# A planned hybrid decoder step: engine queues modelled as overlapping, ScalarE's order fixed too, raw buffers handed out, and the inner product of two heads taken in one copy

## The chip, the cores and the metric

The kernel runs on one core of one Trainium2 chip. The metric is the device time of one execution in microseconds. Before the change it is 3202.98 us, the median of three runs (3199.14 to 3204.49).

The core has engines that run side by side, each with its own queue that it works off in order: TensorE (PE, matrix multiplication into PSUM), VectorE (DVE), ScalarE (ACT), GpSimd (POOL), and SyncE (SP), which issues DMA transfers here. An instruction waits on semaphores for what it needs of other engines, and everything behind it in the same queue waits with it.

## What is computed

One layer of a decoder with a convolution branch and a recurrent branch, on 2048 prompt rows and 8 sampled sequences of 4 rows each, of width 1024. Cut to what matters here:

```python
h = rmsnorm(x, norm_g)
p = h @ w_in                                   # 1024 x 10368
u = cg * xin                                   # convolution branch, width 3
y_c = bg * (conv_w[0]*u[t-2] + conv_w[1]*u[t-1] + conv_w[2]*u[t]) * silu(zc)
# recurrent branch: 16 heads of 64, token shift by mu, then along the sequence, per head
sa = S @ -kk
S  = S * d + outer(sa, kk * a) + outer(v, k)
y  = S @ r
y_r = (groupnorm(y) * ln_w + ln_b + bonus) * silu(zr)
m = sigmoid(gc) * (y_c @ w_out_c) + sigmoid(gr) * (y_r @ w_out_r)
out = rmsnorm(x + m @ w_o, final_g)
```

The last rows of the convolution, of the shift and the states S are returned as well.

## The kernel before, in words

**Tiles and stages.** The prompt is cut into 4 sets of 512 columns (tokens). The input lies with the features on the partitions as a high and a low part (`XH`, `XL`, fp32r); each weight block of 128 columns is split in the same way into `whl`: ACT casts the raw block `wraw` to the high part, DVE subtracts to get the low part. A projection of one block (`proj`) is then 24 matmuls of up to 512 columns, high by high, low by high and high by low, into the PSUM tile `ip`. These are the main stream of PE, some 11,700 matmuls. The split weights are stored to DRAM the first time and loaded split afterwards. A last stage computes the output projections (tiles `RH`, `RL`, `MH`, `ML`, `po`).

**The recurrence in chunks.** Heads are treated in pairs, with head 0 on partitions 0 to 63 and head 1 on 64 to 127. For each of 8 pairs and each set, the 512 tokens are 8 chunks of 64. Within a chunk, the recurrence is solved with the inverse of a triangular matrix per head. `rwkv_solve` finds inverses of 32x32 blocks by 62 short DVE operations (tiles `tt`, `X`, `Mi`), and `rwkv_merge` puts them together in `Xbd`, which before is block-diagonal: head h on rows 64h and columns 64h. `rwkv_chain` then goes through the chunks one after another. For each chunk:

1. PE: `pa` = the state `S` times `AR`.
2. DVE, two operations of 64x64: `us` = `pa` + `P1`, one for each head, stacked on the rows in a tile of 128x64.
3. PE: `pb[:, 0, 0:64]` = `Xbd` times `us`. Head 0 comes out on partitions 0 to 63 and head 1 on 64 to 127.
4. `inner`: DVE copies head 0 into `SV[0:64, c, 0:64]`, and ACT copies head 1 into `SV[0:64, c, 64:128]`.
5. PE: `pb[:, 1]` = `BKt` times `SV`.
6. DVE, two operations: the new `S`. ACT has scaled the old one into `sp` meanwhile.

Each step needs the one before it, and the next chunk needs `S`. There are 4 x 8 x 8 = 256 such chunks.

**What sets the order.** The chains, inverses, key computations and so on are generators, called sides (`Side`), which a driver mixes into PE's main stream: after each main matmul, `drive` asks each side to go on. A side gives out its next step when a model of the engines says that its inputs are ready (`self.due <= clock.t["PE"]`). This model is `Clock`: `add` gives each instruction a start and an end, from costs in `Traced.cost`, from when its inputs are ready, and from a gap in its engine's list of busy times (`gap`). At the end of the first stage the instructions of the engines in `PLANNED`, DVE alone before, are sorted by the starts that the model gave, and are tied together in that order. On the other engines the instructions stand as the framework lists them.

**Buffers.** `wraw` is a ring of 4 buffers of 512 KB, used in turn for raw weights, for rows of `x` and some more. `tmp` is a ring of 8 that are freed by name, and the model takes the one that it expects to be free first. Early in the program, `late_setup` brings the rows of `x` of the later sets through the `wraw` ring, while the first weights come through it too.

Of the kernel before, what the change touches and what calls it, by code (L numbers as in the profile page):

```python
# [16 lines left out]
P = 128  # L17
# [30 lines left out]
PLANNED = ('DVE',)  # L48


class Clock:
# [3 lines left out]
    def __init__(self):  # L55
        self.t = dict.fromkeys(("PE", "DVE", "ACT", "POOL", "SP"), 0.0)
        self.log, self.home = {}, {}
        self.mode = (128, 128)
        self.busy = {"DVE": [], "ACT": [], "POOL": []}
        self.touched = {}  # L60
        self.begun, self.planning = {}, False
        self.held = {"DVE": [], "POOL": []}
# [11 lines left out]
    def pool(self, pool, name, bufs):  # L74
# [9 lines left out]
        def free(k):  # L84

            return max((e[5] for i in range(k) for e in self.log.get(f"{name}{(n[0] + i) % bufs}", ())), default=0.0)
# [39 lines left out]
    def add(self, eng, outs, ins, cost, lag=60.0):  # L126
        start = max([self.t["PE"] - PAST if eng in self.busy else self.t[eng]] + [e[4] for ap in ins for e in self._hits(ap) if e[6] != eng] +
                    [e[5] for ap in (*ins, *outs) for e in self._hits(ap) if e[6] == eng] +
                    [self.touched.get((eng, ap.tensor.name), 0.0) for ap in (*ins, *outs)] +
                    [e[5] for ap in outs for e in self._hits(ap)])  # L130
        if eng in self.busy:
            start = self.gap(eng, start, cost)
        if eng == "POOL" or eng == "DVE" and sum(ap.space != PSUM for ap in ins) > 1:
            for _ in range(3):
# [4 lines left out]
                start = self.gap(eng, start, cost)  # L139
# [6 lines left out]
        if eng in self.busy:  # L146
# [4 lines left out]
            b.insert(i, (start, end))  # L151
            del b[:-200]
        self.t[eng] = max(self.t[eng], end)
        for ap in ins:
            for e in self._hits(ap):
                e[5] = max(e[5], end)
        for ap in outs:
            for p0, p1, f0, f1 in self.boxes(ap):
                old = self.log.setdefault(self.name(ap), [])
                old[:] = [e for e in old if not (p0 <= e[0] and e[1] <= p1 and f0 <= e[2] and e[3] <= f1)][-95:]  # L160
                old.append([p0, p1, f0, f1, end + lag, end, eng, start])
        return start


class Ring:
# [9 lines left out]
    def tile(self, shape, dtype, name, bufs=None):  # L175
        if name != "tmp":
            home, t = name, self.pool.tile(shape, dtype, name=name, bufs=bufs)
        else:
            home = min(self.open, key=self.ends)
# [4 lines left out]
        self.clock.log[home] = [[0, P, -1 << 40, 1 << 40, at, at, None, at]]  # L184
# [8 lines left out]
class Pooled:  # L193
# [3 lines left out]
    def tile(self, shape, dtype, name, bufs=None):  # L197
# [4 lines left out]
        if log:  # L202
            at = max(e[5] for e in log)
            self.clock.log[home] = [[0, P, -1 << 40, 1 << 40, at, at, None, at]]
        return t


class Traced:
# [5 lines left out]
    def __getattr__(self, op):  # L214
        f = getattr(self.eng, op)

        def call(*a, **k):
# [8 lines left out]
            if self.clock.planning and self.name in PLANNED:  # L226
# [4 lines left out]
    def cost(self, op, out, ins, k):  # L231
# [24 lines left out]
        if self.name == "DVE":  # L256
            per = {"transpose": 1.12 if n <= 256 else 1.86, "tensor_tensor_scan": 2.1, "reciprocal": 6.1}.get(op, 1.05)
            if op == "tensor_reduce":
                n = ins[0].free_size()
            one = op == "scalar_tensor_tensor" and isinstance(k["scalar"], bass.AP)  # L260
            return 145 + per * n + 58 * one
        if self.name == "ACT":
            strided = n > 64 and list(ins[0].ap)[-1][0] > 1
            return (155 if ins[0].space == PSUM else 190) + (1.9 if strided else 0.84) * n + 100 * max(0, len(ins) - 1) + 30.0
# [32 lines left out]
def hybrid_kernel(tc, x_prompt, x_sample, state_conv, state_shift, state_rwkv, norm_g, w_in, conv_w,  # L297
# [26 lines left out]
    wraw_p = clock.pooled(ctx.enter_context(tc.tile_pool(name="wraw", bufs=4)), "wraw", 4)  # L324
# [17 lines left out]
    def w_advance(dma, split, load):  # L342
        while state["dma"] < min(dma, len(order)):
            _, src, _, there = order[state["dma"]]
            if not there:
                raw = wraw_p.tile([P, NB * P], F32, name="wraw")
# [79 lines left out]
    class Side:  # L426
# [15 lines left out]
        def run(self, upto, force=False):  # L442
            if any(not x.ended for x in self.after) or upto < self.f0:
                return
            goal = weight[self.kind] * (upto - self.f0) / max(1e-9, self.f1 - self.f0) if upto < self.f1 else float("inf")
            while self.given < goal and self.f0 <= upto and (force or max(self.due, pt_free(self.banks)) <= clock.t["PE"] and (
                    self.kind in URGENT or clock.load("DVE") < BACKLOG)):
                try:
                    x = next(self.g)
                    x, aps, self.banks = (x + ((), 0)[len(x) - 1:]) if isinstance(x, tuple) else (x, (), 0)  # L450
# [3 lines left out]
                    self.due = clock.ready(aps) if aps else 0.0  # L454
                except StopIteration:
                    weight[self.kind] = self.given
# [3 lines left out]

    def need(*sides):
# [28 lines left out]
    def load_x(i):  # L490
        xt = wraw_p.tile([P, D], F32, name="wraw")
# [28 lines left out]
    tmp = Ring(ph1.enter_context(tc.tile_pool(name="tmp", bufs=1)), [P, NT + 64], 8, clock)  # L520
    ep = clock.pooled(ph1.enter_context(tc.tile_pool(name="ep", bufs=2)), "ep", 2)
# [13 lines left out]
    XB = [xp.tile([P, NC1, P], F32, name=f"Xbd{i}") for i in range(2)]  # L535
    SV = xp.tile([P, NC1, P], F32, name="SV")
# [1232 lines left out]
```

## Time and profile before

| | before |
|---|---|
| median of three runs | 3202.98 us |
| the profiled execution, its own time | 3202.88 us |
| its span in the trace | 3201.2 us |
| mean granted clock of TensorE | 0.993 |
| bytes moved by DMA | 615.07 MB, 192 GB/s over the span |
| first stage, to the last chunk of the recurrence | about 2640 us of the span |

The program records every operation through one helper, so nearly all rows of the profile carry the line L218, and a row is told from another by its tiles: `pb<-us,Xbd` is the matmul that writes `pb` from `us` and `Xbd`. An f32 matmul of the kernel is two passes in the trace, so 256 chunks show as 512 rows. "PEld" is the weight load, which runs beside the matmuls. A wait such as "PE pb <- ACT SV" means that PE stood idle before a matmul into `pb` until ACT had written `SV`.

### The profile page before, as it was taken

The page shows a single profiled execution, that of the slowest core. Times are in us where ns is not written, and L with a number is a line of the kernel's source. Part 1 is how long each engine was busy: PE and PEld are TensorE (multiplying, and loading weights), DVE is VectorE, ACT ScalarE, POOL GpSimd, SP SyncE. Part 2 cuts the span into 40 slices and gives each one's busy share as a digit, 9 for nine tenths or more (in the row PEclk, how much of TensorE's full clock was granted, in tenths as well). Part 3 has the DMA queues.
Part 4 walks back from the last instruction along what each step waited for, and adds up shares of the span by engine and source line. Part 5 has one row for each costly group of instructions (what it writes and reads, how often), then busy time and mean ns, then how long its engine had stood idle before and what let it go on. Part 6 is the DMA issues. An engine that isn't in the chain of part 4 may idle for free.

```text
span 3201.2 us, 55474 instructions
## 1 busy us (share of the span) xinstructions
PE 3095.1 (97%) x21530; PEld 2598.3 (81%) x21530; DVE 2000.1 (62%) x5704; ACT 1251.9 (39%) x2571; POOL 312.7 (10%) x517
## 2 busy tenths in 40 slices
PE   7899999999999999999999989999999999999998
PEld 6677777887777778777777789989899988877896
DVE  5677787866666666665666666777677763443332
ACT  5454555444443443444434334334444442311201
POOL 2011111011111111111111110000000000000000
PEclk9999999999999999999999999999999999999999
DMA  7776777654444444444444444334443468988863
GB/s 252 237 238 219 223 230 243 218 178 155 153 158 161 159 159 150 169 159 154 160 154 160 157 133 147 134 124 141 139 147 124 147 217 306 358 327 317 317 243 120
DMA packets 241501, 615.07 MB, mean 192 GB/s; under 512 B 33930, under 2 KB 143619, under 8 KB 187478
## 3 DMA queue, kind: packets, MB, share of 16 engines
q1 hardware_dynamic: 241094, 611.00, 55.9%
q8 instruction: 170, 2.79, 0.4%
q14 instruction: 93, 0.76, 0.1%
q0 software_dynamic: 144, 0.52, 0.0%
HBM read 452.10 MB, written 159.36 MB: 191 GB/s over the span
## 4 chain that ended last, share of the span: by engine, by line
PE 71%; DVE 16%; ACT 4%; issue 4%; DMA 4%; POOL 1%; SPq 0%; ACTq 0%; DVEq 0%; POOLq 0%
PE ip L218 51%; PE pt L218 10%; PE po L218 6%; DVE tt L218 3%; DVE X L218 3%; PE pb L218 3%; ACT tmp L218 2%; DVE Mi L218 2%; DVE tmp L218 2%; PE pa L218 1%; DVE us L218 1%; DVE S L218 1%; DMA wraw<-in_w_in_dram 1%; DVE whl L218 1%; ACT Xbd L218 1%
## 5 line engine op out<-in xcount | busy, mean ns | idle before, releaser
L218 PE MATMUL ip<-XH,whl 128*128 128x512 f32 (+3 forms) x7776 | 2106.6, 351 | 32.0 <-DVE whl L218 14.0
L218 PEld LDWEIGHTS ip<-XH,whl 128*128 128x128 f32 x7776 | 1341.3, 190 | 204.1 <-issue 39.4
L218 PE MATMUL ip<-XL,whl 128*128 128x512 f32 (+3 forms) x3888 | 1363.6, 351 | 2.4 <-DVE XL L218 2.0
L218 PEld LDWEIGHTS ip<-XL,whl 128*128 128x128 f32 x3888 | 738.7, 190 | 80.0 <-issue 7.7
L218 DVE TENSOR_TENSOR X<-X,tt 128x60 f32<-128x60 f32 (+24 forms) x992 | 213.2, 215 | 33.8
L218 DVE TENSOR_TENSOR tt<-Mi,X 128x60 f32<-128x60 f32 (+24 forms) x992 | 213.3, 215 | 27.5
L218 DVE SCALAR_TENSOR_TENSOR S<-pb,pe,sp 64x64 f32<-64x64 f32 x512 | 144.0, 281 | 108.5 <-PE pb L218 103.0
L218 ACT ACTIVATE sp<-S,pe 128x128 f32<-128x128 f32 x256 | 100.0, 401 | 244.5 <-DVE S L218 243.4
L218 ACT ACTIVATE tmp<-ip,vec 128x512 f32<-128x512 f32 (+2 forms) x174 | 103.2, 593 | 229.4 <-PE ip L218 228.0
L218 DVE TENSOR_TENSOR us<-pa,P 64x64 f32<-64x64 f32 x512 | 110.3, 215 | 127.7 <-PE pa L218 118.0
L218 PE MATMUL po<-whl,MH 128*128 128x512 f32 x544 | 170.3, 394 | 0.0
L218 ACT COPY SV<-pb 64x64 f32<-64x64 f32 x256 | 53.6, 209 | 292.7 <-DVE SV L218 290.8
L218 DVE TENSOR_TENSOR whl<-wraw,whl 128x1024 fp32r<-128x1024 f32 x105 | 130.9, 1248 | 20.7 <-ACT whl L218 20.4
L218 ACT CAST whl<-wraw 128x1024 fp32r<-128x1024 f32 x105 | 109.5, 1045 | 82.7 <-DMA wraw<-in_w_out_r_dram 45.1
L218 PEld LDWEIGHTS pb<-SV,BKt 128*128 128x128 f32 x512 | 81.3, 188 | 64.2 <-ACT SV L218 58.7
L218 PE MATMUL ip<-RH,whl 128*128 128x512 f32 (+2 forms) x512 | 128.4, 341 | 1.2 <-DMA whl<-w_or 0.9
L218 PE MATMUL pb<-SV,BKt 128*128 128x128 f32 x512 | 111.2, 299 | 17.5 <-ACT SV L218 16.6
L218 PEld LDWEIGHTS po<-whl,MH 128*128 128x128 f32 x544 | 102.2, 188 | 23.8
L218 DVE TENSOR_TENSOR GM<-pt,mask_p 128x512 f32<-128x512 f32 x128 | 82.5, 686 | 59.3 <-PE pt L218 59.2
L218 PEld LDWEIGHTS pb<-us,Xbd 128*128 128x128 f32 x512 | 86.5, 188 | 35.4 <-PE ip L218 17.0
L218 DVE SCALAR_TENSOR_TENSOR gt<-gt,ip 128x288 f32<-128x288 f32 (+2 forms) x67 | 36.5, 544 | 116.7 <-PE ip L218 102.7
L218 PE MATMUL po<-whl,ML 128*128 128x512 f32 x272 | 107.1, 394 | 0.0
(494 smaller groups left out, 3862.5 us busy)
## 6 DMA issues: line engine op xcount, KB each, us to landing
wraw<-in_w_in_dram SPq DMA_DIRECT2D x81, 512.0 KB
whl<-w_k SPq DMA_DIRECT2D x24, 1024.0 KB
whl<-w_r SPq DMA_DIRECT2D x24, 1024.0 KB
whl<-w_v SPq DMA_DIRECT2D x24, 1024.0 KB
whl<-w_z SPq DMA_DIRECT2D x24, 1024.0 KB
whl<-w_xin SPq DMA_DIRECT2D x24, 1024.0 KB
whl<-w_cg SPq DMA_DIRECT2D x24, 1024.0 KB
whl<-w_zc SPq DMA_DIRECT2D x24, 1024.0 KB
```

Source lines behind the costliest of these rows:

```text
L218: r = f(*a, **k)
```

## The change

Five things change.

- **The model of the queues.** `OVERLAP` lets an instruction of DVE or ACT occupy its engine for less than its duration when its output begins at partition 0, and for more when it does not. The wait for another engine before a buffer is overwritten gets 60 ns; that for the own engine's result is `e[4] - 26`. Some costs of `Traced.cost` change (ACT loses 30 ns; DVE's `tensor_scalar` from SBUF is 0.587 ns an element).
- **The fixed order.** `PLANNED` now holds ACT as well. Operations of the kinds in `LOOSE` (the preparation of `x`, the late setup, and the subtraction of the low part of a weight) are no longer tied, on either engine.
- **Buffers.** `Raws` hands out the four `wraw` buffers by name, as `tmp` is; they are freed where their last reader has been recorded. When no `tmp` is open, `push` forces sides on.
- **The chain.** `Xbd` holds the inverses of both heads in columns 0 to 63, head h still on rows 64h. `us` becomes block-diagonal, in two fixed tiles `UB` of 128x128 whose other blocks stay zero. The product then gives both heads on partitions 0 to 63 in 128 columns, and one ACT copy of 64x128 replaces the DVE copy and the ACT copy of 64x64. The samples' `inner` stays as it was.
- **Small things.** `rst` becomes bf16, and the last rows for `new_shift_p` are handled later in `prep`.

```diff
-PLANNED = ('DVE',)
+PLANNED = ('DVE', 'ACT')
+LOOSE = ('prep', 'first', 'late', 'zero', 'low')
+OVERLAP = {"DVE": (83, 13), "ACT": (60, 18)}
...
     def add(self, eng, outs, ins, cost, lag=60.0):
...
-                    [e[5] for ap in (*ins, *outs) for e in self._hits(ap) if e[6] == eng] +
+                    [e[4] - 26.0 if eng in OVERLAP else e[5] for ap in (*ins, *outs) for e in self._hits(ap) if e[6] == eng] +
                     [self.touched.get((eng, ap.tensor.name), 0.0) for ap in (*ins, *outs)] +
-                    [e[5] for ap in outs for e in self._hits(ap)])
+                    [e[5] + 60.0 * (e[7] != eng) for ap in outs for e in self._hits(ap)])
+        took = cost
+        if eng in OVERLAP:
+            over, drain = OVERLAP[eng]
+            p0 = self.boxes(outs[0])[0][0]
+            took = cost - over if p0 == 0 else cost + over + 2 * drain
         if eng in self.busy:
-            start = self.gap(eng, start, cost)
+            start = self.gap(eng, start, took)
...
+class Raws:
+    def __init__(self, pool, size, n, clock):
+        self.pool, self.clock, self.size = pool, clock, size
+        self.open, self.out = [f"wraw{i}" for i in range(n)], {}
...
+    def tile(self):
+        home = min(self.open, key=self.ends)
+        self.open.remove(home)
+        t = self.pool.tile([P, self.size], F32, name="wraw", tag=home)
...
-            if self.clock.planning and self.name in PLANNED:
+            if self.clock.planning and self.clock.kind not in LOOSE and self.name in PLANNED:
                 self.clock.begun.setdefault(self.name, []).append((at, r.ins))
...
-    wraw_p = clock.pooled(ctx.enter_context(tc.tile_pool(name="wraw", bufs=4)), "wraw", 4)
+    wraw_p = Raws(ctx.enter_context(tc.tile_pool(name="wraw", bufs=1)), NB * P, 4, clock)
...
+            was, clock.kind = clock.kind, "low"
             V.tensor_tensor(out=hl[:, 1], in0=raw, in1=hl[:, 0].bitcast(F32), op=ALU.subtract)
+            clock.kind = was
+            wraw_p.free(raw)
...
+    def push():
+        for sd in [sd for kind in ("samp", "keys", "out") for sd in live if sd.kind == kind and sd.f0 <= where[0]]:
+            if all(x.ended for x in sd.after):
+                sd.run(where[0] + 1e-6, True, True)
+                if tmp.open:
+                    return
...
+    UB = [xp.tile([P, P], F32, name=f"UB{i}") for i in range(2)]
...
-    rst = con.tile([P, NT], F32, name="rst")
+    rst = con.tile([P, NT], BF16, name="rst")
...
+    col = [slice(32 * b, 32 * b + 32) for _ in range(2) for b in range(2)]
...
-            A.copy(Xbd[g, 0:NCH, g].rearrange("p c (a e) -> p c a e", e=4),
+            A.copy(Xbd[g, 0:NCH, col[i]].rearrange("p c (a e) -> p c a e", e=4),
...
-                us = sm.tile([P, 64], F32, name="us")
+                us = UB[c % 2]
                 for h in range(2):
-                    V.tensor_tensor(out=us[HS[h]], in0=pa[0:64, c - g, HS[h]], in1=P1[HS[h], c, :], op=ALU.add)
+                    V.tensor_tensor(out=us[HS[h], HS[h]], in0=pa[0:64, c - g, HS[h]], in1=P1[HS[h], c, :], op=ALU.add)
...
-                inner(c, pb[:, 0], us, Xbd)
+                T.matmul(pb[:, 0, :], lhsT=Xbd[:, c, :], rhs=us, start=True, stop=True)
+                A.copy(SV[0:64, c, :], pb[0:64, 0, :])
```

Three places show what this does to the order. The first is PE's queue in the chain of the second set, some 1004 us into the program, from the product with the inverse (`pb<-us,Xbd`, afterwards `pb<-UB,Xbd`) to the next product of that chunk (`pb<-SV,BKt`). Before:

```order
2980 L218 MATMUL pb<-us,Xbd_209 128x64
2981 L218 MATMUL ip<-XH,whl 128x512 x2
2982 L218 MATMUL ip<-XL,whl 128x512
2983 L218 MATMUL ip<-XH,whl 128x512 x2
2984 L218 MATMUL ip<-XL,whl 128x512
2985 L218 MATMUL ip<-XH,whl 128x512
2986 L218 MATMUL pb<-SV,BKt 128x128
```

The same chunk in the changed program:

```order
2966 L264 MATMUL pb<-UB_210,Xbd_209 128x128
2967 L264 MATMUL ip<-XH,whl 128x512 x2
2968 L264 MATMUL ip<-XL,whl 128x512
2969 L264 MATMUL ip<-XH,whl 128x512 x2
2970 L264 MATMUL ip<-XL,whl 128x512
2971 L264 MATMUL pb<-SV,BKt 128x128
```

Six main matmuls stand between the two products where there were seven. The right side is 128 columns wide instead of 64.

The second place is ACT's queue at the same chunk; `cv<-u,cwh` is a step of the convolution that needs `u` from DVE, and `sp<-S,pe` is the scaling of the old state. Before:

```order
725 L218 ACTIVATE tmp<-tmp 128x512
726 L218 COPY SV<-pb 64x64
727 L218 ACTIVATE sp<-S_474,pe 128x128
728 L218 ACTIVATE cv<-u,cwh 128x512
729 L218 COPY SV<-pb 64x64
730 L218 ACTIVATE sp<-S_474,pe 128x128
```

In the changed program:

```order
729 L264 ACTIVATE tmp<-tmp 128x512
730 L264 ACTIVATE sp<-S_476,pe 128x128
731 L264 COPY SV<-pb 64x128
732 L264 ACTIVATE cv<-u,cwh 128x512
733 L264 ACTIVATE sp<-S_476,pe 128x128
```

The copy of this chunk (the second `SV<-pb` of the first list) has moved from behind the convolution's step to ahead of it.

The third place is DVE's queue in the first set, during the first inverse, where the low part of a weight is made (`whl<-wraw,whl`). Before, at the end of the inverse:

```order
149 L218 TENSOR_TENSOR tt<-Mi,X 128x24
150 L218 TENSOR_TENSOR X<-X,tt 128x8x3
151 L218 TENSOR_TENSOR tt<-Mi,X 128x16
152 L218 TENSOR_TENSOR X<-X,tt 128x8x2
153 L218 TENSOR_TENSOR tt<-Mi,X 128x8
154 L218 TENSOR_TENSOR X<-X,tt 128x8
155 L218 TENSOR_TENSOR whl<-wraw,whl 128x1024
156 L218 STREAM_TRANSPOSE Xo<-X 128x256
```

In the changed program, in the middle of that inverse:

```order
125 L264 SCALAR_TENSOR_TENSOR kT<-ip,omu,tmp 128x512
126 L264 TENSOR_TENSOR tt<-Mi,X 128x65
127 L264 TENSOR_TENSOR whl<-wraw,whl 128x1024
128 L264 TENSOR_TENSOR X<-X,tt 128x5x13
129 L264 TENSOR_TENSOR tt<-Mi,X 128x60
130 L264 TENSOR_TENSOR X<-X,tt 128x5x12
131 L264 TENSOR_TENSOR tt<-Mi,X 128x66
132 L264 TENSOR_TENSOR whl<-wraw,whl 128x1024
```

The subtraction, no longer tied to a planned place, has moved from behind the whole inverse into it.

Over the whole program the counts by operation are the same but for these: 256 DVE copies `SV<-pb` are gone, 256 ACT copies `SV<-pb` are 64x128 instead of 64x64, 256 matmuls into `pb` have 128 columns instead of 64, and POOL sets two tiles `UB` to zero at the start.

More of the change, by code (lines that the diff above doesn't have):

```diff
@@ L138, in add @@
                         start = e
-                start = self.gap(eng, start, cost)
+                start = self.gap(eng, start, took)
                 if start == was:
@@ L150, in add @@
                 i -= 1
-            b.insert(i, (start, end))
+            b.insert(i, (start, start + took))
             del b[:-200]
@@ L178, in tile @@
         else:
+            for _ in range(60):
+                if self.open:
+                    break
+                self.push()
             home = min(self.open, key=self.ends)
@@ L259, in cost @@
                 n = ins[0].free_size()
+            if op == "tensor_scalar" and ins[0].space != PSUM:
+                per = 0.587
             one = op == "scalar_tensor_tensor" and isinstance(k["scalar"], bass.AP)
@@ L699, in prep @@
                 to_cols(q, xt, (i - th * TPS) * P, G if k % 2 else V)
+                if q == NB // KG - 1 and i < NTL - 1:
+                    wraw_p.free(xt)
                 yield 1
@@ L717, in late_setup @@
             stat_tile(i, xt, m)
+            if i < NTL:
+                wraw_p.free(xt)
             yield 1
```

77 lines of the change are left out of this document (52 added, 25 removed).

## The prediction

> **What bounds the kernel now.** I read the page first, for the busy shares and the chain that ended last.
>
> ```profile
> span 3201.2 us, 55474 instructions
> PE 3095.1 (97%) x21530; PEld 2598.3 (81%) x21530; DVE 2000.1 (62%) x5704; ACT 1251.9 (39%) x2571; POOL 312.7 (10%) x517
> ...
> PE 71%; DVE 16%; ACT 4%; issue 4%; DMA 4%; POOL 1%; SPq 0%; ACTq 0%; DVEq 0%; POOLq 0%
> ```
>
> TensorE is busy for 97% of the span, so 106 us of it are open idle time (3201.2 - 3095.1). No other engine comes near. Whatever gains here must take work from PE or let it wait less. The program's count of matmuls does not change, so it comes down to waits. A busy PE can hide part of a wait, because pipelined matmuls overlap in the records; the weight loads therefore belong beside it. The view of the waits, for the matmuls and for the weight loads:
>
> ```profile
> PE pb L218 <- ACT SV L218: 16.6, 42, 2.1
> PE ip L218 <- DVE whl L218: 14.0, 6, 6.1
> ...
> PE pb L218 <- DVE us L218: 6.9, 21, 0.4
> ...
> PE pa L218 <- DVE S L218: 1.4, 2, 1.1
> PEld pb L218 <- ACT SV L218: 58.7, 140, 2.5
> ```
>
> Each row gives the total in us, how often, and the longest. The recurrence's chain is the largest single cause: for 140 of its 256 chunks the weights `SV` come late, 58.7 us together, of which 16.6 us are open idle time of PE. Next is the wait for a weight's low part, 14.0 us in six places, one of them of 6.1.
>
> What such a late `SV` costs is seen in one chunk of the timeline (start, duration, engine, instruction; "x2" are two passes or two matmuls):
>
> ```profile
> 1002.67 0.40 PE L218 MATMUL ip<-XL,whl 128*128 128x512 f32 x1
> 1002.90 0.38 PE L218 MATMUL pa<-S,AR 128*128 128x128 f32 x2
> 1003.04 0.71 PE L218 MATMUL ip<-XH,whl 128*128 128x512 f32 x2
> 1003.59 0.40 PE L218 MATMUL ip<-XL,whl 128*128 128x512 f32 x1
> ...
> 1004.53 0.33 PE L218 MATMUL pb<-us,Xbd 128*128 128x64 f32 x2
> 1004.66 0.71 PE L218 MATMUL ip<-XH,whl 128*128 128x512 f32 x2
> 1004.82 0.68 DVE L218 TENSOR_TENSOR u<-ip,tmp 128x512 f32<-128x512 f32 x1
> 1005.21 0.39 PE L218 MATMUL ip<-XL,whl 128*128 128x512 f32 x1
> ...
> 1005.42 0.21 DVE L218 COPY SV<-pb 64x64 f32<-64x64 f32 x1
> ...
> 1005.54 0.73 ACT L218 ACTIVATE cv<-u,cwh 128x512 f32<-128x512 f32 x1 [3.46 <-DVE u L218]
> ...
> 1006.14 0.40 PE L218 MATMUL ip<-XH,whl 128*128 128x512 f32 x1
> 1006.17 0.20 ACT L218 COPY SV<-pb 64x64 f32<-64x64 f32 x1
> ...
> 1006.41 0.30 PEld L218 LDWEIGHTS pb<-SV,BKt 128*128 128x128 f32 x2 [0.31 <-ACT SV L218]
> 1006.41 0.49 PE L218 MATMUL pb<-SV,BKt 128*128 128x128 f32 x2
> ...
> 1006.66 0.48 PE L218 MATMUL ip<-XH,whl 128*128 128x512 f32 x1
> ```
>
> The product `pb<-us,Xbd` ended at 1004.86 (1004.53 + 0.33). DVE was in `u` and copied only at 1005.42. ACT then took `cv<-u`, which its queue had ahead and for which it had stood idle 3.46 us, and copied at 1006.17. PE began at 1006.41 and the next main matmul at 1006.66. An undisturbed step takes 0.23 from the main matmul before it (1002.67 to 1002.90) and 0.14 to the one behind (1002.90 to 1003.04); here these are 0.27 and 0.25. So a wait of 0.31 in the weight load cost PE 0.15, and about 0.16 of each wait is hidden. Over all 140: 58.7 - 140 x 0.16 = 36 us lost, my estimate, between the bounds 16.6 and 58.7.
>
> **The change part by part.** The sum is made against the profiled execution's own 3202.88 us, which is the median (3202.98) within 0.1 us.
>
> *The copy of SA.* The groups of the two copies, and of a wider copy from PSUM on ACT:
>
> ```profile
> L218 DVE COPY SV<-pb 64x64 f32<-64x64 f32 x256 | 52.8, 206 | 57.7 <-PE pb L218 57.6
> L218 ACT COPY SV<-pb 64x64 f32<-64x64 f32 x256 | 53.6, 209 | 292.7 <-DVE SV L218 290.8
> L218 ACT COPY BKt<-pt 128x128 f32<-128x128 f32 x8 | 2.1, 267 | 0.1
> ```
>
> ACT's copy follows DVE's: its idle time ends with DVE's copy for 290.8 of 292.7 us. The change removes 256 copies of 206 ns from DVE and from the step, and widens ACT's from 64 to 128 columns, 209 to at most 267 ns: 0.15 us a step shorter. The planner gives that back: on PE's queue shown with the change, six main matmuls stand where seven stood, 0.23 us less cover. So the shorter step is worth nothing by itself; what counts is that one queue fewer can be late. In the chunk above, DVE's lateness was 0.56 us (1004.86 to 1005.42) and ACT's 0.54 (1005.63 to 1006.17). The first goes with the DVE copy; the second goes where the fixed order of ACT puts the copy ahead of `cv`, as its queue now has it. ACT is busy 39% of the time against DVE's 62%, so what is late next is an ACT evacuation of up to 0.6 us ahead of the copy. I take two thirds of 36 us as gained: **-24**, between 0 (all given back) and -58.7.
>
> *The right side, 128 instead of 64 columns.* In the timeline above, `pa` with 128 columns and `us` with 64 can be compared: from the first pass to the start of the third main matmul behind it, `pa` takes 1002.90 to 1003.59 = 0.69 and `us` 1004.53 to 1005.21 = 0.68, each with two main matmuls in it. So the wider side costs 0.01 a chunk, **0** (at most 3 us over 256). Its upper bound is the pass itself: the two passes' common duration is 0.38 against 0.33, the second pass starting 0.05 later; if both passes paid this, 256 x 2 x 0.05 = 26 us.
>
> *The sums `us` on DVE.* Their number and size stay, two 64x64 operations. The waits for them:
>
> ```profile
> L218 PEld LDWEIGHTS pb<-us,Xbd 128*128 128x128 f32 x512 | 86.5, 188 | 35.4 <-PE ip L218 17.0 <-issue 6.4 <-DVE us L218 0.3
> ```
>
> PE loses between 6.9 us (its idle row above) and 35.4. DVE has 52.8 of 2000.1 us less to do, and the planner's starts for DVE change with the overlap. I take **-4**, with +10 to -20 as ends, since a new order can also be a worse one.
>
> *The low part of a weight, and the raw buffers.* This is the 6.1 us wait:
>
> ```profile
> 110.83 0.39 PE L218 MATMUL pa<-S,AR 128*128 128x128 f32 x2
> ...
> 116.05 1.22 DVE L218 TENSOR_TENSOR whl<-wraw,whl 128x1024 fp32r<-128x1024 f32 x1
> ...
> 117.33 0.80 PE L218 MATMUL ip<-XH,whl 128*128 128x512 f32 x1 [6.11 <-DVE whl L218]
> 117.92 0.63 PE L218 MATMUL ip<-XL,whl 128*128 128x512 f32 x1
> 118.35 1.05 PE L218 MATMUL ip<-XH,whl 128*128 128x512 f32 x2
> 119.20 0.63 PE L218 MATMUL ip<-XL,whl 128*128 128x512 f32 x1
> 119.63 1.05 PE L218 MATMUL ip<-XH,whl 128*128 128x512 f32 x2
> 120.48 0.43 PE L218 MATMUL ip<-XL,whl 128*128 128x512 f32 x1
> 120.75 0.63 PE L218 MATMUL ip<-XH,whl 128*128 128x512 f32 x2
> ```
>
> DVE made this low part only when the whole inverse was through, since its fixed order had it there; and after the wait PE runs at about half speed to 120.75: eight main matmuls from 117.33 take 3.42 us, where 8 x 0.23 = 1.84 is usual, so 1.6 us more. With the change the low part stands in the middle of the inverse. Of 6.1 + 1.6 us I take **-6**. The raw buffers themselves I cost at nothing: they decide when a load may start, and the weights' loads keep their rank before the rows of `x` in SP's queue or gain one. If a row of `x` now holds a weight back there, the six waits of 14.0 us double; so +14 to -14.
>
> *ACT's fixed order elsewhere.* Weight loads also wait for other ACT results; the longest are 8.3 us for `tmp` and 7.5 for `Wm`. I take **-2**, with the sign open:
>
> ```profile
> PEld pt L218 <- ACT tmp L218: 8.3, 19, 1.4
> ...
> PEld pt L218 <- ACT Wm L218: 7.5, 20, 0.7
> ```
>
> `rst` in bf16, two POOL memsets and the later `new_shift_p` lie beside PE's stream, on engines at 62% and 10%; without that cover they are a few us at most.
>
> Sum: -24 + 0 - 4 - 6 - 2 = -36, and 3202.88 - 36 = **3167 us**.
>
> **The rivals.** *The planner takes it all back.* It places the product as soon as its model says that `SV` is ready, so a shorter step brings an earlier product and as many waits. The 0.23 taken from the cover speaks for this; the two lateness terms of the chunk, which the model did not foresee, speak against. Left are the 6 us at the start: 3197, and up to 3204.
>
> *All waits of the chain go.* Two queues foreseen well would free PE of nearly everything: -45 for `SV`, -15 for `us`, -10 at the start, -6 elsewhere: 3127. Against it stands DVE, still 60% busy and still in two steps of three.
>
> *Slower: ACT's queue is blocked by a weight.* The 81 casts of raw blocks of `w_in` (1.05 us each) are ACT instructions of the main stream and are tied now. Such a cast waits for a DMA, whose landing the model only guesses. Where the block is late, the copies `SV` and the evacuations of `ip` queue behind it and PE stops within the six matmuls of cover. It decides from a mean lateness of 36 / 81 = 0.44 us per cast on; at 0.7 us it is +57 - 36, or 3224. The trace of before shows ACT waiting long for a raw block only where the last stage begins:
>
> ```profile
> ACT whl L218 <- DMA wraw<-in_w_out_r_dram: 45.1, 2, 39.3
> ```
>
> *The wide side costs what its columns cost.* At the bound of 26 us the forecast becomes 3193. The two distances of 0.69 and 0.68 speak against it. A rule that says the same: the Trainium skill, "TensorE: Matmul & The Clock Gate", section "Back-to-back issue gap", gives about 60 cycles for up to 64 columns and 134 for 128, and "FP8 and Floating Point Precision", section "TensorE Precision Notes", four passes for full fp32; an estimate from these is 74 cycles at 2.4 GHz x 4 x 256 = 32 us, or 3199. The trace disagrees as far as it goes, since `pa` already has 128 columns at no more than `us` with 64.
>
> **How the numbers follow.** Forecast (3150 to 3185): 0.56. Planner takes it back: 0.17. All waits go: 0.12. ACT blocked: 0.09. Width costs: 0.06. A measurement of this kernel can tell about 0.2% from no change, which is 3196.6 to 3209.4. Faster is the forecast, all waits, half of the planner's case and most of the width's: 0.80; the same 0.11; slower 0.09, nearly all from ACT. The range has to hold eight in ten: up to 3204, the planner's upper end, and down to 3138, which takes in part of the larger gain and leaves the slower case out.
>
> **What would show it.** Right, if the weight loads' wait for `SV` falls from 58.7 to about 20 us with some 50 waits, the 6.1 us wait near 117 us is below 3, and the distance from `pb<-UB,Xbd` to the third main matmul behind it stays at 0.68 to 0.69. The planner's case shows as a wait for `SV` that stays near 58.7. The blocked case shows as ACT idle before `whl` on a DMA in the first stage, followed by waits of PE for ACT. The width's case shows in the distance alone. The forecast is wrong if DVE's new order makes the waits for `us` or `S` grow by more than what `SV` gives.

## The result and the profile after

The changed kernel takes 3172.86 us, the median of four runs (3170.4 to 3176.81), against 3203.57 us of the kernel before in the same comparison: a ratio of 0.9906, with a 95% interval of 0.9895 to 0.9918, some 31 us faster. The forecast was 3167 us. The profiled execution took 3173.76 us, with a span of 3172.0 us and a mean granted clock of 0.992, so the clock (0.993 before) does not explain the gain.

The page of the changed kernel, its busy shares and the chain that ended last:

```profile
span 3172.0 us, 55351 instructions
PE 3076.3 (97%) x21530; PEld 2605.9 (82%) x21530; DVE 1964.8 (62%) x5448; ACT 1249.5 (39%) x2571; POOL 313.5 (10%) x519
```

PE's open idle time is 3172.0 - 3076.3 = 95.7 us; it was 106. So only 10 of the 29 us of span come from idle time that a row names. Most of the rest lay in waits that overlapping records of PE cover up, which is why the weight loads have to be read too.

The waits of the changed kernel, for matmuls and for weight loads (total us, times, longest):

```profile
PE ip L264 <- DVE tmp L264: 14.7, 8, 8.0
PE pt L264 <- DVE T L264: 11.6, 22, 1.4
...
PE ip L264 <- DVE whl L264: 5.2, 5, 3.3
...
PE pb L264 <- DVE UB L264: 2.9, 8, 0.8
```

```profile
PEld pt L264 <- DVE T L264: 20.5, 40, 1.7
...
PEld pb L264 <- ACT SV L264: 3.1, 10, 0.6
```

The weight loads' wait for `SV` is 3.1 us in 10 places, where it was 58.7 in 140. The low part `whl` fell from 14.0 to 5.2, and `UB` is at 2.9 where `us` had 6.9. Two waits are new or larger: the matmuls `pt<-T,...` of the merge wait for DVE's transposed tile `T` (the weight loads 20.5 us in 40 places, before 8.1 in 20), and the wait for `tmp` grew from 8.4 to 14.7, of which 8.0 lie in one place.

The prediction followed one chunk in which `cv<-u` stood ahead of the copy. The same chunk in the timeline of the changed kernel:

```profile
993.70 0.68 DVE L264 TENSOR_TENSOR u<-ip,tmp 128x512 f32<-128x512 f32 x1
993.75 0.38 PE L264 MATMUL pb<-UB,Xbd 128*128 128x128 f32 x2
993.89 0.71 PE L264 MATMUL ip<-XH,whl 128*128 128x512 f32 x2
994.17 0.26 ACT L264 COPY SV<-pb 64x128 f32<-64x128 f32 x1 [2.87 <-PE pb L264]
994.41 0.72 ACT L264 ACTIVATE cv<-u,cwh 128x512 f32<-128x512 f32 x1
994.44 0.39 PE L264 MATMUL ip<-XL,whl 128*128 128x512 f32 x1
...
995.37 0.39 PE L264 MATMUL pb<-SV,BKt 128*128 128x128 f32 x2
995.51 0.71 PE L264 MATMUL ip<-XH,whl 128*128 128x512 f32 x2
```

DVE is in `u` again when the product ends at 994.13, but nothing of the step is queued behind it now. ACT copies 0.04 us after the product's end and takes `cv<-u` afterwards. The product with `SV` starts without a wait, 0.14 us ahead of the next main matmul, as in an undisturbed step. From the product with the inverse to the third main matmul behind it are 0.69 us (993.75 to 994.44), with 128 columns.

Where the time was saved along the program shows when the same main matmul is looked up in both traces (start after minus start before, us):

```
main matmul     500  1500  2000  4000  6000  6500  9500 10500 11000   end
after-before  -10.6 -10.3  -3.9 -12.5 -15.2 -24.3 -30.5 -40.1 -30.1 -29.4
```

The last column is the start of PE's last record; the whole span is 29.1 us shorter. Ten us come at the start, of which 6 go again between matmuls 1500 and 2000; some 36 come along the rest of the recurrence, and ten are lost between matmuls 10500 and 11000, where the last stage begins.

To compare whole kernels, I took the distance from each of PE's matmul records to the next, subtracted the tenth percentile that this pair of tiles (with its columns) has over all kernels compared, and put the excess down to the later tile. The sum of the excess and of the subtracted base is the distance from the first to the last record:

```
us                 before   after  chain   plan no_pin  no_ov chain_t after_t after_c after_tc
pb<-SV,BKt           45.5     6.9   24.6   19.1   20.5   10.4    24.9     6.9     9.0      8.0
pb<-us or UB,Xbd     23.2    17.9   18.5   28.1   20.0   25.3    21.0    21.1    18.5     20.4
pt<-T,Mo              3.4    24.5   28.4   15.1   25.5   26.0     8.4     3.6    24.7      4.5
pt<-T,GM             10.0     5.3    7.2    7.9   15.2   11.2    27.0    11.6    10.6     13.3
pa<-S,AR              7.0    11.8   13.9   12.0   13.3    9.9    11.5    12.3    12.5     13.3
ip<-XH,whl          121.5   125.6  127.4  124.5  103.8  120.6   127.9   129.6   105.9    105.5
all excess          465.9   442.7  475.0  460.6  440.7  467.7   480.5   435.9   433.4    414.2
base               2719.6  2713.4 2719.9 2718.5 2711.5 2711.0  2719.4  2711.3  2711.9   2711.8
```

The columns behind `after` are the experiments below, in the order chain_only, plan_only, no_pin, no_overlap, chain_t, after_t, after_cast, after_t_cast.

### The profile page after: what moved, and what is told of

Same layout as the page of the kernel before. It is cut to its first block, busy times and chain, and to the rows that moved or that the text cites. A ratio compares the mean times of both kernels' runs of the same rounds, so it can differ in the third digit from the quotient of the medians.

```text
span 3172.0 us, 55351 instructions
## 1 busy us (share of the span) xinstructions
PE 3076.3 (97%) x21530; PEld 2605.9 (82%) x21530; DVE 1964.8 (62%) x5448; ACT 1249.5 (39%) x2571; POOL 313.5 (10%) x519
## 4 chain that ended last, share of the span: by engine, by line
PE 55%; DVE 15%; issue 4%; DMA 2%; ACT 1%; POOL 0%; SPq 0%; DVEq 0%; ACTq 0%; POOLq 0%
PE ip L264 39%; PE pt L264 7%; PE po L264 6%; DVE tt L264 4%; DVE X L264 4%; PE pb L264 2%; PE pa L264 1%; DVE S L264 1%; DVE tmp L264 1%; DVE Yc L264 1%; ACT Xbd L264 1%; DMA tmp<-gc 1%; DMA gc<-tmp 1%; DVE UB L264 0%; ACT tmp L264 0%
## 5 line engine op out<-in xcount | busy, mean ns | idle before, releaser
L264 ACT COPY SV<-pb 64x128 f32<-64x128 f32 x256 | 66.2, 259 | 324.7 <-PE pb L264 323.2
L264 DVE TENSOR_TENSOR UB<-pa,P 64x64 f32<-64x64 f32 x512 | 110.3, 215 | 98.8 <-PE pa L264 92.9
L264 ACT COPY Xbd<-Xo 32x256 f32<-32x256 f32 x128 | 87.4, 682 | 70.1 <-DVE Xo L264 68.1
L264 PEld LDWEIGHTS pb<-UB,Xbd 128*128 128x128 f32 x512 | 86.5, 188 | 29.0 <-issue 8.6
L264 PEld LDWEIGHTS pa<-S,AR 128*128 128x128 f32 x512 | 89.3, 189 | 24.6 <-DVE S L264 10.0
```

Of the source, the lines that this page charges most:

```text
L264: r = f(*a, **k)
```

## The experiments

### The parts of the change, one at a time

Four kernels take the change apart. The first is the kernel before with the chain's change alone (and `rst` in bf16, for the room):

```diff
+    UB = [xp.tile([P, P], F32, name=f"UB{i}") for i in range(2)]
-            A.copy(Xbd[g, 0:NCH, g].rearrange("p c (a e) -> p c a e", e=4),
+            A.copy(Xbd[g, 0:NCH, col[i]].rearrange("p c (a e) -> p c a e", e=4),
...
-                us = sm.tile([P, 64], F32, name="us")
+                us = UB[c % 2]
...
-                inner(c, pb[:, 0], us, Xbd)
+                T.matmul(pb[:, 0, :], lhsT=Xbd[:, c, :], rhs=us, start=True, stop=True)
+                A.copy(SV[0:64, c, :], pb[0:64, 0, :])
```

> The kernel before with the chain's change alone (stacked inverses, block-diagonal right side, one copy; the bf16 rst makes the room that the two UB tiles need). Old model, ACT not tied, old wraw ring. Theory A (the wait for SV came half from DVE's copy being late and half from ACT's free order): the weight loads' wait for SV falls from 58.7 us to 20 to 35, time 3203 - 12 to - 18 = 3185 to 3191, ratio about 0.995. Theory B (the better model of the queues does it): the wait stays above 45 us, time within 5 us of before. Theory C (the lost DVE copy alone does it): the wait is below 10 us, time 3203 - 22 to - 30 = 3173 to 3181.

The second is the changed kernel with the old chain put back, so that the queues' model, the fixed order of ACT and the buffers remain:

```diff
-                us = UB[c % 2]
+                us = sm.tile([P, 64], F32, name="us")
...
-                T.matmul(pb[:, 0, :], lhsT=Xbd[:, c, :], rhs=us, start=True, stop=True)
-                A.copy(SV[0:64, c, :], pb[0:64, 0, :])
+                inner(c, pb[:, 0], us, Xbd)
```

> The changed kernel with the old chain put back (stacked us of 64 columns, DVE copy and ACT copy); new model, ACT tied, buffers handed out, low part loose. Theory A: wait for SV 20 to 35 us, time 3203 - 14 to - 20 = 3183 to 3189. Theory B: wait below 10 us, time 3173 to 3180, as the changed kernel. Theory C: wait above 45 us, time 3190 to 3200, the 6 us at the start and a little more.

The third and the fourth change one line each of the changed kernel, `PLANNED = ('DVE',)` and `OVERLAP = {}`.

> The changed kernel with ACT no longer tied to the planned order (DVE alone, as before). Theory A: the wait for SV rises from 3.1 to 12 to 20 us, time 3173 + 8 to + 14 = 3181 to 3187. Theories B and C: the wait stays below 6 us and the time within 4 us of the changed kernel's 3173.

> The changed kernel without the model of overlapping queues (OVERLAP empty, so an instruction occupies its engine for its whole cost and a result of the own engine counts from its end); the other changes of costs stay. Theories A and C: wait for SV below 10 us, time within 5 us of 3173, either way. Theory B: wait for SV above 30 us and time 3190 or more. If the new waits for T (11.6 us of PE) and S (3.9 us) come from this model, they go here.

| kernel | median us | kernel before, same chip | ratio, 95% interval |
|---|---|---|---|
| chain_only | 3214.74 | 3205.11 | 1.0035 [1.0023, 1.0048] |
| plan_only | 3198.62 | 3205.11 | 0.9981 [0.9971, 0.9990] |
| no_pin | 3176.32 | 3205.11 | 0.9912 [0.9899, 0.9924] |
| no_overlap | 3195.27 | 3205.11 | 0.9970 [0.9958, 0.9981] |

The parts don't add: the chain alone makes the kernel 10 us slower, the plan alone 6 us faster, and together they give 31. The waits of chain_only:

```profile
PE pt L218 <- DVE T L218: 20.8, 20, 2.2
...
PE pb L218 <- ACT SV L218: 9.9, 25, 1.6
```

```profile
PEld pb L218 <- ACT SV L218: 26.3, 49, 2.0
PEld pt L218 <- DVE T L218: 22.8, 21, 2.3
```

The shorter step does what was forecast of it, since `SV` falls from 58.7 to 26.3; in the table of excess this is 45.5 to 24.6. But the new order brings the merge forward too: the wait for `T` comes up with 20.8 us of open idle time, and `pt<-T,Mo` costs 25 us more. In the changed kernel the first product of the merge, `pt<-T,Mo`, stands 15 main matmuls earlier than before in twelve of the 16 merges of the second and third set, and PE waits 0.5 to 0.6 us at each of these. In chain_only the same twelve stand 19 earlier, and PE waits 0.7 to 1.0 us at each. In plan_only the weight loads wait for `SV` 19.9 us:

```profile
PEld pb L264 <- ACT SV L264: 19.9, 43, 1.6
```

```profile
PE pb L264 <- DVE us L264: 9.5, 26, 0.9
PE pb L264 <- ACT SV L264: 6.1, 9, 1.2
```

Only in the whole change is `SV` at 3.1. Without the overlap 22 us of the gain go, spread over `us`, `T` and the transposes of `BK` (15.5 us of excess against 3.3). Without ACT's fixed order the time is the same within the intervals: `SV` costs 13.6 us more (20.5 against 6.9), `pt<-T,GM` 10 more, and `ip<-XH,whl` 22 less. So the fixed order helps the copies and costs about as much elsewhere; a later section asks where.

None of the theories written down for these four runs held whole. chain_only had theory A's wait (26.3 us) without its time, and plan_only 19.9 us of wait with theory C's time. no_pin had a wait a little above theory A's (22.5 us) with the time of B and C, 3.5 us from the changed kernel. no_overlap had the wait of A and C (9.1 us) with B's time.

### What the wide right side costs

The kernel before, with `us` in two fixed tiles, and in one of two runs the product issued with all 128 columns, whose right half is zero and unused. The planner counts 64 columns in both. The control has the order of the kernel before on PE, DVE and ACT; with the wide side the order there differs by a few neighbours exchanged, and so does that of the transfers at the last stage.

```diff
-            r = f(*a, **k)
+            r = f(*a, **{**k, **(self.clock.wide or {})})
...
-                us = sm.tile([P, 64], F32, name="us")
+                us = UB[c % 2][:, 0:64]
...
+        clock.wide = wide is not None and dict(out=pb, rhs=wide)
-        T.matmul(pb[:, 0:64], lhsT=Xbd[:, c, :], rhs=us, start=True, stop=True)
+        T.matmul(out=pb[:, 0:64], lhsT=Xbd[:, c, :], rhs=us, start=True, stop=True)
+        clock.wide = None
```

> The kernel before, with the sums us in two fixed tiles (left half, 64 columns) and rst in bf16, all else and the order of every queue as before. Both theories: the time of before, ratio 0.999 to 1.001. It is the comparison for the run with the wide right side.

> As the control, but the right side of the product pb<-UB,Xbd is 128 columns wide (the right half is zero and its result is not used); the planner counts 64, and but for a few neighbours exchanged the order of PE, DVE and ACT is the same. Theory W0 (the width costs nothing, since the distance of main matmuls around the product is set by the weight loads): within 3 us of the control. Theory W1 (each of the two passes pays its 0.05 us): +26 us. Theory W2 (74 cycles on each of four passes): +32 us. Waits for SV should stay near 58.7 us by W0, and grow by some 256 x 0.05 us if the later end of the pass holds the copies back.

The control took 3206.33 us, a ratio of 1.0001 [0.9992, 1.0010], and the wide one 3211.73 us, 1.0017 [1.0008, 1.0026]: 5.4 us between them, outside the 3 us of the first theory and far from the 26 and 32 of the others. (The two profiled executions are 3.3 us apart.) One product with 64 columns in the control, and one with 128:

```profile
1008.06 0.33 PE L219 MATMUL pb<-UB,Xbd 128*128 128x64 f32 x2
1008.20 0.71 PE L219 MATMUL ip<-XH,whl 128*128 128x512 f32 x2
1008.75 0.39 PE L219 MATMUL ip<-XL,whl 128*128 128x512 f32 x1
```

```profile
1005.64 0.38 PE L219 MATMUL pb<-UB,Xbd 128*128 128x128 f32 x2
1005.78 0.71 PE L219 MATMUL ip<-XH,whl 128*128 128x512 f32 x2
1006.33 0.39 PE L219 MATMUL ip<-XL,whl 128*128 128x512 f32 x1
```

The main matmul behind starts 0.14 us after the product in both, and the third at 0.69; the medians over the chunks are the same. So PE's queue pays nothing. The product itself ends 0.05 us later, and that shows where the step is late already. The weight loads' wait for `SV`, control first:

```profile
PEld pb L219 <- ACT SV L219: 56.6, 137, 2.5
```

```profile
PEld pb L219 <- ACT SV L219: 62.4, 137, 2.5
```

137 waits at 0.05 us would be 6.9; the rows differ by 5.8, and the excess of `pb<-SV,BKt` by 6.9 (44.0 to 50.9). The time of the pair is no clean measure of this, though. The wide run also loses 3.4 us after main matmul 10500, where no chunk is left. There its transfer queue has five loads of `gc` behind a weight load, and PE waits 6.1 us, where the control waits 1.5 us:

```profile
2685.62 0.33 SPq L290 DMA_DIRECT2D whl<-w_oc  x1
2685.99 2.62 SPq L290 DMA_DIRECT2D tmp<-gc  x5
2691.68 0.79 PE L219 MATMUL ip<-XH,whl 128*128 128x256 f32 x2 [6.09 <-DVE tmp L219]
```

If each execution loses these 3.4 us, 2 of the 5.4 are left, and the first theory is not refuted. So the width costs some 2 to 7 us here, an estimate from these rows. In chain_only, 49 steps are late for `SV`; at 0.05 us each, its wide product explains at most 2.5 of the 10 us lost, by this estimate. The rest stands beside the new wait for `T` and is not isolated.

### The new wait for T

The timeline of the changed kernel at a merge (the inverses `Xo` are copied into `Xbd` by ACT, DVE transposes 32x32 blocks into `T`, and PE multiplies with them):

```profile
1032.54 2.81 ACT L264 COPY Xbd<-Xo 32x256 f32<-32x256 f32 x4 [1.60 <-DVE Xo L264]
1033.14 0.74 DVE L264 SCALAR_TENSOR_TENSOR kT<-ip,omu,tmp 128x512 f32<-128x512 f32 x1
1033.80 0.42 DVE L264 STREAM_TRANSPOSE T<-Xbd 32x256 f32<-32x256 f32 x1
...
1034.82 0.43 DVE L264 STREAM_TRANSPOSE T<-Xbd 32x256 f32<-32x256 f32 x1
...
1035.31 0.21 PE L264 MATMUL pt<-T,Mo 32*32 32x32 f32 x1 [0.55 <-DVE T L264]
```

PE stands idle for 0.55 us before this matmul until the second transpose is through. My theory: the planner counts on `T` some 0.9 us too early, since the inverse ahead of it runs longer than its costs say. The trace fits: the inverse's dependent operations on `tt` and `X` follow each other 14 ns later on average than the model's cost and gap give, and 62 x 14 ns is 0.87 us. To test it, the model is told that `T` comes 0.9 us later, once in chain_only and once in the changed kernel:

```diff
+        for e in clock._hits(T11[0:96]):
+            e[4] += 900.0
```

> chain_only, with the model told that the tile T of the merge is ready 0.9 us later than it thinks, so that PE's first product of the merge stands some main matmuls later. chain_only cost 10 us although its waits for SV fell by 21; theory D: that gain was eaten by PE's new wait for T (0.3 to 0.4 us idle before, 20.8 us with the chain alone), because the planner places the merge by an inverse that it thinks shorter than it is. Then the wait for T falls below 5 us here and the time by 15 to 25 us against chain_only, to 3190 to 3200. Theory E (the wide right side costs PE time that no wait shows): T's wait falls but the time stays above 3208.

> The changed kernel with the same 0.9 us for T. Theory D: PE's wait for T falls from 11.6 us to below 3, pt<-T together some 15 us less, time 3173 - 8 to - 16 = 3157 to 3165. Rival: the PE order shifts elsewhere and waits as much for something else, time within 4 us of 3173.

In the changed kernel it holds: 3162.38 us, a ratio of 0.9871 [0.9855, 0.9888], 10 us better, and `pt<-T,Mo` falls from 24.5 to 3.6 us. In chain_only it fails: 3219.89 us, 1.0049 [1.0037, 1.0062], no faster and rather slower. There the wait for `T` fell as well, but others came in its place, as the waits of chain_t show:

```profile
PE pt L218 <- ACT SV L218: 15.2, 12, 1.3
...
PE pt L218 <- DVE T L218: 5.8, 5, 2.1
```

PE now stands before matmuls into the merge's `pt`, and the excess of `pt<-T,GM` rises from 7.2 to 27.0. The `SV` that it waits for is not the chain's copy but a copy of 64x512 out of another `pt`, which in ACT's queue stands behind the four copies into `Xbd`:

```profile
1048.85 2.78 ACT L218 COPY Xbd<-Xo 32x256 f32<-32x256 f32 x4 [1.37 <-DVE Xo L218]
...
1051.64 0.58 ACT L218 COPY SV<-pt 64x512 f32<-64x512 f32 x1
...
1052.27 0.21 PE L218 MATMUL pt<-T,GM 32*32 32x32 f32 x1 [1.26 <-ACT SV L218]
```

In after_t both such copies are through before the copies into `Xbd` begin (1029.5 against 1031.16 us).

Both `pt<-T` rows together cost 35.4 us in chain_t and 35.6 in chain_only; in after_t they cost 15.2, against 29.8 in the changed kernel. My second theory was that this takes a planned order on ACT, which copies `Xbd` ahead of `T`. The test is the later `T` with ACT's order not fixed, the one line `PLANNED = ('DVE',)` in after_t:

> The changed kernel with ACT's order not fixed (as no_pin, 3176.3) and T told 0.9 us later (as after_t, 3162.4). Theory A (the later T is worth something only where ACT, which copies Xbd ahead of T and evacuates the merge behind it, keeps to the planned order): no gain over no_pin, 3173 to 3182, with pt<-T,Mo and pt<-T,GM together as large as in no_pin. Rival (the queues' overlap in the model is what chain_t lacked; ACT's order doesn't matter): 10 us gained, 3166, and both rows together 20 us or more smaller.

The theory falls: 3168.51 us, a ratio of 0.9880 [0.9864, 0.9897], against 0.9912 [0.9899, 0.9924] of no_pin, and both rows together fall from 40.7 to 21.9 us (5.7 and 16.2). The medians gain 7.8 us and the rows 18.8, a little less than the rival's 10 and 20, and 8.2 us come back at the merge's next products, `pt<-Xbd,Wm` (12.7 to 20.9), which wait for ACT's `Wm`. The profiled execution of no_pin_t is itself 3 us longer than that of no_pin, so the gain is that of the medians; the traces show only where the waits moved. ACT's fixed order is thus not what chain_t lacked. What remains between chain_t and this kernel is the model of the queues with its overlap and costs, the untied kinds and the buffers; which of them makes the later `T` pay was not tried apart.

### The casts of raw weights, and the low part

The prediction's slower rival was that ACT's tied casts of raw weights wait for DMA and block the copies. Here the casts alone are left untied, first with the later `T`, then without it:

```diff
+                was, clock.kind = clock.kind, "low"
                 A.copy(hl[:, 0], raw)
+                clock.kind = was
```

> after_t, with the casts of raw weights to their high part no longer tied on ACT. Without any tie on ACT the waits for SV rose by 14 us but PE's waits before main matmuls fell by about 22 in that run. Theory F: it was the casts that the tie makes late; then SV stays below 6 us of wait, PE's waits on whl and before main matmuls fall, time 5 to 12 us below after_t. Rival (the difference between the two runs lay at the stage's end by chance): time within 4 us of after_t.

> The changed kernel, with only the ACT casts of raw weight blocks no longer tied to the planned order (no later T). Theory P (a tied cast holds up the copies behind it in ACT's queue, independent of T): 15 us less than the changed kernel, 3158, the same step as from 3162.4 to 3147.3 with the later T. Rival (the gain came only together with the later T, as another order drawn): within 5 us of 3173.

With the later `T` the kernel takes 3147.32 us, a ratio of 0.9827 [0.9811, 0.9844], and beats both kernels; that is 15 us below after_t, more than the 5 to 12 expected. Without it 3162.61 us, 0.9869 [0.9855, 0.9882], which is 10 us better than the changed kernel and not the 15 expected; nor is it the rival's 5 or less. Its mechanism is not the one I had written down either: with the casts untied, `SV` costs 9.0 us instead of 6.9, so no copy had been held up. The row of the casts in the first stage of the changed kernel (to 2560 us; busy us, mean ns, idle time before them and what ended it):

```profile
L264 ACT CAST whl<-wraw 128x1024 fp32r<-128x1024 f32 x82 | 85.3, 1041 | 7.6 <-DMA wraw<-in_w_in_dram 7.4
```

7.4 us over 82 casts are 0.09 us each, far from the 0.44 from which the rival decides. Between main matmuls 10500 and 11000, at the last stage, the changed kernel loses 10.0 us, after_cast gains 4.4, and no_pin 1.3. The timeline there, of the changed kernel and then of after_cast (SPq is the queue that issues the transfers):

```profile
2640.82 0.28 PE L264 MATMUL ip<-XL,whl 128*128 128x256 f32 x1
2641.13 0.33 SPq L337 DMA_DIRECT2D whl<-w_oc  x1
2641.50 2.58 SPq L337 DMA_DIRECT2D tmp<-gc  x5
2648.59 1.09 DVE L264 SCALAR_TENSOR_TENSOR tmp<-tmp,ip 128x256 f32<-128x256 f32 x3 [10.71 <-DMA tmp<-gc]
2649.06 0.80 PE L264 MATMUL ip<-XH,whl 128*128 128x256 f32 x2 [7.97 <-DVE tmp L264]
```

```profile
2635.61 2.62 SPq L337 DMA_DIRECT2D tmp<-gc  x2
...
2642.27 0.32 SPq L337 DMA_DIRECT2D whl<-w_oc  x1
2643.21 1.10 DVE L264 SCALAR_TENSOR_TENSOR tmp<-tmp,ip 128x256 f32<-128x256 f32 x3 [4.18 <-DMA tmp<-gc]
2643.69 0.50 PE L264 MATMUL ip<-XH,whl 128*128 128x256 f32 x2 [1.45 <-DVE tmp L264]
```

In the changed kernel the loads of `gc` are issued right behind a weight load `whl<-w_oc`, which goes out as PE ends the matmul at 2640.82 + 0.28. They land some 7 us later; DVE needs them for `tmp`, and PE stands for 8.0 us. Behind that wait PE's granted clock is 0.50 (2649.0 to 2652.4), which adds to the loss. In after_cast they go out ahead of the weight load, 6 us earlier, and PE waits 1.45. So the difference lies at the last stage, in another order of its transfers.

Whether the tie *causes* this order is open. Among the eight kernels built from the changed one, itself included, the late order goes with the tied casts: the four that tie them (the changed kernel, plan_only, no_overlap, after_t) lose 7.3 to 10.0 us between these matmuls, and the four that don't (no_pin, no_pin_t, after_cast, after_t_cast) lose nothing. But chain_only, chain_t, low_loose and wide_only, which tie nothing on ACT, also issue five loads of `gc` right behind `whl<-w_oc`; PE waits 7.9, 8.0, 9.3 and 6.1 us at the same main matmul, and they lose 4.6, 6.0, 3.6 and 2.6 us in this stretch. So the tie alone does not decide it, and no run moves these loads by themselves.

The last experiment is the kernel before with only the subtraction of the low part untied on DVE:

```diff
+            clock.kind = 'low'
             V.tensor_tensor(out=hl[:, 1], in0=raw, in1=hl[:, 0].bitcast(F32), op=ALU.subtract)
+            clock.kind = None
```

> The kernel before, with nothing changed but that the subtraction of a weight's low part is not tied on DVE. The prediction's step on the start: the 6.1 us wait near 117 us falls below 3 and the time by 6 us, to 3199 (5 to 9 less). Rival: the gain at the start came from the raw buffers' new order instead; then the wait stays and the time is within 2 us of before.

It took 3200.27 us against 3204.11, a ratio of 0.9988 [0.9979, 0.9997]. Its waits:

```profile
PE ip L220 <- DVE tmp L220: 16.5, 10, 9.3
...
PE ip L220 <- DVE whl L220: 3.3, 1, 3.3
```

`whl` falls by 10.7 us, from 14.0 to 3.3, and the long wait near 117 us is gone, so the untied subtraction does this without the new raw buffers. The gain of 3.8 us is below the 5 to 9 expected: the wait for `tmp` takes 8.1 us back (16.5 against 8.4), with a piece of 9.3 that is the late `gc` at the last stage.

## Why the prediction held, step by step

The forecast of -36 us measured -31 in the medians, and -29.1 in the profiled spans. Taken singly, its terms were less good than their sum.

- **The copy of SA, -24.** Right in direction and mechanism, too small in size: 45.5 - 6.9 = 38.6 us of excess went, well above the two thirds of 36 that I took. I expected a wait of about 20 us in 50 places to remain, and 3.1 in 10 did. One reading was wrong: `SV` is the right side of that product, and its weights are `BKt` (`lhsT` in the kernel's call). The wait only stands at the weight load in the records, ahead of the product. What I had feared as late next, an evacuation on ACT ahead of the copy, hardly occurs once ACT's order is planned. That one queue fewer and the plan are both needed is shown by the parts: 24.6 with the chain alone, 19.1 with the plan alone, 20.5 with both but without the fixed order.
- **The planner takes it back.** It did not for `SV`, though the cover shrank from seven main matmuls to six. It did elsewhere: many of the inverses' merges came forward, and the matmuls with `T` lost 21.1 - 4.7 = 16.4 us (`pt<-T,Mo` and `pt<-T,GM`). This term was missing from my sum; so was `pa<-S,AR`, which lost 4.8 us (7.0 to 11.8). The row `PEld pt <- DVE T`, 8.1 us in 20 places before, was there to be asked what happens to the next planned wait; I had only asked it of the chain. Telling the model of 0.9 us more gained 10 us.
- **The right side, 0.** On PE's queue 0.69 us before and after, as forecast. The direct test shows what the forecast left out: a result that is 0.05 us later costs some 2 to 7 us where the step is late in 137 of 256 chunks. In the changed kernel, with 10 such waits left, this has little to act on. The rule from the Trainium skill that was weighed there ("TensorE: Matmul & The Clock Gate", section "Back-to-back issue gap") gave 32 us as an estimate. That section of the Trainium skill states the gap for an isolated matmul. The measured 5.4 us, with 0.14 us to the next matmul at either width, speaks against using it for a product between main matmuls.
- **The sums `us`, -4.** 23.2 to 17.9, or -5.3. The wait of the matmuls fell from 6.9 to 2.9.
- **The low part, -6.** The 6.1 us wait near 117 us is gone, and by main matmul 500 the changed kernel is 10.6 us ahead. Untied alone it is worth 6.6 us by main matmul 500 and 3.8 us of the whole time.

At the corresponding place of the changed kernel's timeline, two shorter waits stand where the long one stood:

```profile
103.78 0.50 PE L264 MATMUL ip<-XH,whl 128*128 128x512 f32 x1 [2.23 <-ACT whl L264]
...
105.04 0.80 PE L264 MATMUL ip<-XH,whl 128*128 128x512 f32 x1 [0.76 <-DVE whl L264]
```

- **ACT's fixed order elsewhere, -2 with the sign open.** With the casts tied it is about +10, and the loss lies at the last stage. The blocked case as I described it (casts waiting for DMA in the first stage, copies behind them) did not occur; the loss showed in a queue that I had not asked about, SP's, and that the tie causes it is not shown.

In sum: some 15 us more than forecast came from `SV`, and 16 went to `T` and 10 to the last stage, with small gains between. These errors nearly cancelled. The mechanism of the main term was right; that the time was met within 6 us is luck of the sum.

## What to carry to other kernels

A planned order that becomes tighter in one place meets the next estimate that is too early; list the waits that are already there for a planned result, and ask of each what it becomes when everything ahead of it moves up. A cheaper dependent step pays only with a planner that places it well: here the step alone was worth +10 us, the planner alone -6, and both -31. And before an engine's instructions are tied to a planned order, ask of each kind whether its input comes from a transfer, and look at the order of the transfer queue in the program that comes out. Here that order was worth up to 10 us, with ties and without.

## What was not expected of the hardware

A 128-column f32 product and a 64-column one take the same room between main matmuls, 0.14 us to the next and 0.69 to the third, while the wider one ends 0.05 us later. In the one direct test the cost showed where steps were late already, as 6.9 us of excess at the product with `SV`. The waits in weight loads counted more than expected: 58.7 - 3.1 = 55.6 us fewer of them came with 38.6 us less excess at that matmul, 0.69 of it, where PE's own idle rows for `SV` had shown only 16.6.
